# Long-range rows with one maximum, a score bank lent to the projections, and keys in 1024-column tiles

## Chip, cores and metric

The kernel runs on one core of a Trainium2 chip. The metric is device time in microseconds (us) for one execution, lower is better. A time is the median of several runs. A profile is one execution taken by the hardware profiler; its span runs from the first to the last instruction. Engines: PE is TensorE (PEld its weight loads), DVE VectorE, ACT ScalarE, POOL GpSimd, SP SyncE. In this kernel SP issues every DMA.

## What is computed

One layer of a streaming encoder in fp32, for 2048 prompt tokens and 32 sample tokens (with a cache of 128), width 1024. After a norm, one projection gives two groups of attention. Group A ("long-range" here) is differential attention: 4 heads, two query/key maps of 64, values of 128.

```python
s = jnp.einsum('bqhmd,bkhmd->bhmqk', q, k) * (HEAD_DIM ** -0.5) + bias[:, None]
s = jnp.where(mask, s, NEG)
p = jax.nn.softmax(s, axis=-1)
w = p[:, :, 0] - lam * p[:, :, 1]
return jnp.einsum('bhqk,bkhe->bqhe', w, v)
```

The mask is causal by chunks of 64. The bias depends on the distance alone and, once its value for far distances is taken off (softmax does not see it), is zero beyond the last 256 keys of a block of 128 queries. Group B (band) has 8 heads of 64, each chunk attending to itself and 8 chunks before. Then follow an output projection, an MLP of 4096 with a squared ReLU, a gate from a per-layer embedding, and a last norm. New keys and values are outputs too.

## The kernel before

Every fp32 operand of a matmul is split into a high and a low part (`split`, L176 to L187: ACT writes the high part at L181, POOL, L166 and L176, or DVE the low part), and a product takes three matmuls (`mm3`, L216 to L218). Weights come by DMA as `wr`, their parts are `wh` and `wl`.

The code lists work stage by stage. A scheduler with a timeline model puts each engine's instructions into one fixed order, so work of neighbouring stages is interleaved where data and buffers allow; on the chip each engine then runs its list in order. Tiles come from pools with a fixed number of buffers, and a write to a reused buffer waits for its last reader.

PSUM has eight banks of 128 x 512 fp32. Before the change: `mm`, 2 banks, for projections and MLP (`vps`, `qps`, `ups`, `dps`); `pss`, 3 banks (tag `s`), for scores of both groups (`s` at L638, `sb` at L835); `pst`, 2 banks, for transposes (`tpp`, L713); `pso`, 1 bank, for attention outputs (`o`, L727 to L729).

The order of `run`: token preparation with the first value tiles; query and key projections of group A for tokens 0 to 1023; the first long-range part `JA0` (pairs of query tiles 0 to 3, `self.small` true); projections and band rows for all tokens, and group A's second half; the second long-range part `JA1` (pairs 4 and 5, then 6 and 7 with the samples); output projection, MLP, gate and final norm. In the trace the first long-range part runs between 187 and about 480 us beside projections of group B, the second between 1215 and about 1990 beside output projection and MLP of tokens 0 to 1023.

`attn_a` loops over the 4 heads. For each it loads the bias block `ba` (`bias_a`), and the keys of the head, high and low part on 64 partitions each, into one tile `ka` of 1024 columns (first part) or 2048 (second part) with two buffers; then it calls `attn_a_pair` for each pair of 128-query tiles.

`attn_a_pair` handles the two query tiles, for each of the two maps m:

- The keys are cut into blocks: the last 256 columns are the near block, what lies before it is cut evenly into far blocks of up to 512. For each block two matmuls (high and low part) make the scores.
- A far block: DVE takes the negated maximum out of PSUM (L644), and ACT computes exp out of PSUM into SBUF with the block's own maximum and sum (L652). A near block: DVE adds the bias, writes to SBUF and takes the maximum (L647), flips the sign (L650), and ACT takes the exp from SBUF.
- After all blocks: the least of the negated maxima (L657), a correction factor for each block by an exp on ACT (L659), and five small DVE operations (L662 to L666) that give each block its factor.
- For each block ACT scales map 1's weights (L674) and DVE combines the maps (L675). PE transposes the row, ACT (L720) and DVE (L721) take it out as high and low part, and three matmuls per 128 keys make the output. `e0` has two buffers, `e1` two in the first part and one in the second.

The band rows use three `s` banks, an addition with maximum on DVE (L838) and one exp per row.

Of the kernel before, what the change touches and what calls it, by code (L numbers as in the profile page):

```python
# [13 lines left out]
F32 = mybir.dt.float32  # L14
# [6 lines left out]
P = 128  # L21
D = 1024
SP = 2048
# [120 lines left out]
class Kern:  # L144
# [75 lines left out]
    def rsqrt(self, pool, src, n, scale, eps, eng, tag="rs", np_=P, bufs=None, out=None):  # L220
        nc = self.nc
        v = pool.tile([P, n], F32, tag=tag + "v", bufs=bufs, name="rsv")[:np_]
# [102 lines left out]
    def bias_a(self, pool, h):  # L325
        nc = self.nc
        t = pool.tile([P, 256], F32, tag="ba", bufs=1, name="ba")
        src = self.dba[h, 127 : 127 + P * 383].rearrange("(p c) -> p c", c=383)[:, :256]
        self.dma(t, src)
        nc.gpsimd.memset(t[0:64, 192:256], NEG)  # L330
        return t
# [240 lines left out]
    def attn_a(self, js, pool, ps_s, ps_t, ps_o):  # L572
# [4 lines left out]
        for g in range(4):  # L577
            ba = self.bias_a(pool, g)
            kt = pool.tile([P, 2, 1024 if self.small else SP], F32R, tag="ka", bufs=2, name="ka")
            if last:  # L580
                ks = pool.tile([P, 2, PAST + SS], F32R, tag="ks", bufs=1, name="ks")
            for hl in range(2):
                src = self.kS[g, hl].rearrange("(m r) c -> r m c", m=2)
                for c0 in range(0, nk, 1024):
                    c1 = min(c0 + 1024, nk)
                    self.dma(kt[64 * hl : 64 * hl + 64, :, c0:c1], src[:, :, c0:c1])
                if last:
                    self.dma(ks[64 * hl : 64 * hl + 64], src[:, :, SP:KC])
            for j in js:
                self.attn_a_pair(g, j if j < 8 else None, kt if j < 8 else ks, ba, pool, ps_s, ps_t, ps_o, late)  # L590
                if self.small:
                    late.pop(0)()
# [3 lines left out]
    def attn_a_pair(self, g, j, kt, ba, pool, ps_s, ps_t, ps_o, late):  # L596
# [11 lines left out]
        for qi, t in enumerate(tiles):  # L608
            if samp:
                nr = SS  # L610
                blocks = [(SP, PAST + SS, 0)]
                kb = SP
                nkeys = PAST + SS
            else:
                nr = P
                kb = 0
                nkeys = P * (t + 1)
                nfar = max(nkeys - 256, 0)
                nb = (nfar + 511) // 512
# [8 lines left out]
            e = [  # L628
                pool.tile([P, 2048 if not self.small else 1024], F32, tag=f"e{m}", bufs=2 if m == 0 or self.small else 1, name="e")
                for m in range(2)  # L630
            ]
            nm = pool.tile([P, 2, 8], F32, tag="nm", bufs=2, name="nm")
            z = pool.tile([P, 2, 8], F32, tag="z", bufs=2, name="z")
            for bi, (k0, n, near) in enumerate(blocks):
                for m in range(2):
                    s = ps_s.tile([P, 512], F32, tag="s", name="s")[:nr, :n]
                    for hl in range(2):
                        nc.tensor.matmul(  # L638
                            s, q[:, m, hl, P * qi : P * qi + nr], kt[:, m, k0 - kb : k0 - kb + n], start=hl == 0, stop=hl == 1
                        )  # L640
                    dst = e[m][:nr, k0 - kb : k0 - kb + n]
                    nmx = nm[:nr, m, bi : bi + 1]
                    if near is None:
                        nc.vector.tensor_reduce(nmx, s, axis=AX.X, op=ALU.max, negate=True)  # L644
                        src = s
                    else:
                        nc.vector.tensor_tensor_reduce(  # L647
                            dst, s, ba[:nr, near : near + n], 1.0, -3e38, ALU.add, ALU.max, nmx
                        )
                        nc.vector.tensor_scalar(nmx, nmx, -1.0, None, op0=ALU.mult)  # L650
                        src = dst
                    nc.scalar.activation(dst, src, AF.Exp, bias=nmx, accum_out=z[:nr, m, bi : bi + 1])  # L652
            c = pool.tile([P, 2, 8], F32, tag="c", bufs=2, name="c")
# [1059 lines left out]
```

## Time and profile before

| | |
|---|---|
| median of 3 runs | 3140.01 us (3138.12 to 3142.35) |
| the profiled execution's own time | 3143.18 us |
| its span | 3141.4 us |
| mean granted TensorE clock | 0.984 |
| DMA | 539.27 MB, mean 172 GB/s |

A stage is a window of time; a row of the stage view gives the window, its length, then the busy time of each engine in it with the count of instructions, the granted TensorE clock, the DMA share and the rate. A row of a group view gives line, engine, operation, output and input tiles and count, then busy time and mean ns of one, then how long the engine was idle just before them and what ended that. A row of the wait view reads "waiter <- releaser: us in total, times, longest". Busy matmuls overlap in the pipeline, so a PE at 100% is not PE at its peak rate.

### The profile page before, as it was taken

How to read it: one execution, taken by the hardware profiler on the slowest of the kernel's cores; microseconds unless marked ns; L12 is line 12 of the kernel's file. 1: busy time of each engine (PE TensorE's matmuls, PEld its weight loads, DVE VectorE, ACT ScalarE, POOL GpSimd, SP SyncE). 2: the span in 40 equal slices, each digit the busy share in tenths (PEclk: the TensorE clock that was granted, in tenths of full speed). 3: DMA queues.
4: the chain of work that ended last, by engine and by line, in shares of the span. 5: the costliest groups of instructions: out<-in, count | busy, mean ns of one | idle time of the engine just before them, and what ended most of it. 6: DMA issues, size and time to landing. Idle time of an engine off the chain costs nothing. (4 is left out here: it accounts for less than half of the span.)

```text
span 3141.4 us, 52810 instructions
## 1 busy us (share of the span) xinstructions
PE 3009.3 (96%) x17913; PEld 2651.0 (84%) x17913; DVE 1897.7 (60%) x4596; ACT 1876.7 (60%) x4166; POOL 1841.0 (59%) x2496
## 2 busy tenths in 40 slices
PE   8999898999999999999999999999899999999998
PEld 7787787999977887878788888878788888999998
DVE  5147774645465654676756656435667885576653
ACT  5257775766676764776666657454555455554545
POOL 2357455332345644665655545667877888767674
PEclk9999899999999999999999999999999999999999
DMA  8788757986788746555563543537533446333231
GB/s 275 244 239 249 207 185 231 266 230 202 205 251 231 221 126 155 156 152 151 164 191 116 145 123 109 157 98 247 174 128 115 144 153 227 124 107 107 88 116 56
DMA packets 523286, 539.27 MB, mean 172 GB/s; under 512 B 38748, under 2 KB 401568, under 8 KB 523016
## 3 DMA queue, kind: packets, MB, share of 16 engines
q1 hardware_dynamic: 523016, 535.89, 56.6%
q8 instruction: 142, 2.33, 0.3%
q14 instruction: 128, 1.05, 0.1%
HBM read 421.97 MB, written 117.75 MB: 172 GB/s over the span
## 5 line engine op out<-in xcount | busy, mean ns | idle before, releaser
L176 POOL TENSOR_TENSOR wl<-wr,wh 128x256 fp32r<-128x256 f32 x648 | 474.4, 764 | 360.3 <-ACT wh L181 326.7
L181 ACT ACTIVATE piece<-wr 128x512 fp32r<-128x512 f32 x406 | 245.6, 625 | 270.3 <-PE ups L217 107.1
L176 POOL TENSOR_TENSOR piece<-wr,piece 128x256 fp32r<-128x256 f32 x404 | 327.5, 836 | 101.8 <-ACT piece L181 79.8
L181 ACT ACTIVATE wh<-wr 128x1024 fp32r<-128x1024 f32 x228 | 241.0, 1057 | 175.5 <-PE qps L217 41.3
L166 POOL TENSOR_TENSOR wl<-wr,wh 128x256 fp32r<-128x256 f32 x264 | 198.0, 781 | 196.4 <-ACT wh L181 186.3
L216 PE MATMUL dps<-uh,piece 128*128 128x272 f32 (+1 forms) x768 | 246.4, 324 | 6.7 <-DVE h L1221 2.5
L166 POOL TENSOR_TENSOR piece<-wr,piece 128x256 fp32r<-128x256 f32 x280 | 236.1, 874 | 26.6 <-ACT piece L181 25.5
L218 PE MATMUL dps<-uh,piece 128*128 128x272 f32 (+1 forms) x768 | 247.1, 324 | 1.6 <-POOL piece L166 1.5
L216 PE MATMUL ups<-cs,piece 128*128 128x256 f32 (+1 forms) x864 | 245.7, 285 | 1.6 <-DVE r L1232 1.6
L217 PE MATMUL dps<-ul,piece 128*128 128x272 f32 (+1 forms) x768 | 247.2, 323 | 0.0
L217 PE MATMUL ups<-cs,piece 128*128 128x256 f32 (+1 forms) x864 | 245.7, 285 | 0.0
L218 PE MATMUL ups<-cs,piece 128*128 128x256 f32 (+1 forms) x864 | 245.5, 284 | 0.0
L216 PE MATMUL qps<-aH,wh 128*128 128x512 f32 (+1 forms) x640 | 231.7, 362 | 7.7 <-DVE ql L476 3.8
L218 PE MATMUL qps<-aH,wl 128*128 128x512 f32 (+1 forms) x640 | 229.7, 359 | 0.0
L217 PE MATMUL qps<-aL,wh 128*128 128x512 f32 (+1 forms) x640 | 229.0, 358 | 0.0
L1173 DVE TENSOR_TENSOR h<-h,dps 128x512 f32<-128x512 f32 x256 | 174.2, 682 | 84.9 <-PE dps L218 79.2
L1221 DVE TENSOR_TENSOR h<-h,dps 128x272 f32<-128x272 f32 (+1 forms) x384 | 189.0, 513 | 51.6 <-PE dps L218 50.8
L216 PE MATMUL dps<-uh,wh 128*128 128x512 f32 x512 | 208.7, 408 | 9.6 <-DVE h L1173 5.3
L216 PE MATMUL ups<-cH,wh 128*128 128x512 f32 x512 | 202.8, 396 | 1.8 <-DVE h L1173 1.7
L218 PE MATMUL dps<-uh,wl 128*128 128x512 f32 x512 | 202.3, 395 | 0.0
L217 PE MATMUL dps<-ul,wh 128*128 128x512 f32 x512 | 201.8, 394 | 0.0
L638 PE MATMUL s<-ka,q 128*128 128x512 f32 (+3 forms) x768 | 187.1, 346 | 15.0 <-ACT e L652 7.1
(317 smaller groups left out, 9619.0 us busy)
## 6 DMA issues: line engine op xcount, KB each, us to landing
wr<-w_up SPq DMA_DIRECT2D x128, 512.0 KB, 3.9
wr<-w_down SPq DMA_DIRECT2D x128, 512.0 KB, 3.8
wr<-w_in SPq DMA_DIRECT2D x74, 512.0 KB, 5.5
q<-qS SPq DMA_DIRECT2D x128, 256.0 KB, 5.2
v<-vSa SPq DMA_DIRECT2D x64, 512.0 KB, 4.0
ka<-kS SPq DMA_DIRECT2D x32, 512.0 KB, 8.4
wr<-w_out SPq DMA_DIRECT2D x32, 512.0 KB, 4.5
wr<-w_ple_gate SPq DMA_DIRECT2D x32, 512.0 KB, 4.2
```

What stands on the lines that cost most here:

```text
L166: nc.gpsimd.tensor_tensor(out[:, sl], a[:, sl], b[:, sl], op=op)
L176: nc.gpsimd.tensor_tensor(out[:, sl], a[:, sl], b[:, sl], op=op)
L181: nc.scalar.activation(hi, raw, AF.Copy)
L216: nc.tensor.matmul(ps, lh, rh, start=start and i == 0, stop=False)
L217: nc.tensor.matmul(ps, lh, rl, start=False, stop=False)
L218: nc.tensor.matmul(ps, ll, rh, start=False, stop=stop and i == n - 1)
L638: nc.tensor.matmul(s, q[:, m, hl, P * qi : P * qi + nr], kt[:, m, k0 - kb : k0 - kb + n], start=hl == 0, stop=hl == 1)
L1173: nc.vector.tensor_tensor(hv, hv, ps, op=ALU.add)
L1221: nc.vector.tensor_tensor(hv, hv, ps, op=ALU.add)
```

## The change

1. **One maximum for a long-range row.** Blocks are now cut at multiples of 512. A far block is copied from PSUM to SBUF by one DVE `tensor_scalar` that also takes the maximum; the last block adds the bias as before, over its whole width, so the bias tile `ba` grows to 512 columns, the first 256 zero (one more memset on POOL). A last block of 128 columns is joined with the one before and the two are cut 384 and 256. A small reduction gives the row's maximum, and one exp on ACT per map runs over the whole row in SBUF with one sum. The per-block factors go; the scaling and combining of the maps run over up to 1024 columns at once. The loop now takes all blocks of one map before the next map.
2. **A bank moves.** `pss` gets 2 banks instead of 3; the eighth bank is a third one for the projections (`mmx`) until the second long-range part, where it becomes a third score bank (`psy`). The band rows and the ring of the token preparation use two score banks throughout.
3. **Keys in tiles of 1024 columns.** In the second part a head's keys lie in two tiles of 1024 columns, from three buffers, in place of one tile of 2048 from two. A score block that crosses a tile's edge is made by two pairs of matmuls.
4. `e1` has two buffers in the second part too; the variance tile of a norm shares a buffer with `sq`.

```diff
     def bias_a(self, pool, h):
-        t = pool.tile([P, 256], F32, tag="ba", bufs=1, name="ba")
+        t = pool.tile([P, 512], F32, tag="ba", bufs=1, name="ba")
...
+        self.dma(t[:, 256:512], src)
+        nc.gpsimd.memset(t[:, 0:256], 0.0)
+        nc.gpsimd.memset(t[0:64, 448:512], NEG)
...
-            kt = pool.tile([P, 2, 1024 if self.small else SP], F32R, tag="ka", bufs=2, name="ka")
+            kts = [pool.tile([P, 2, 1024], F32R, tag="ka", bufs=2 if self.small else 3, name="ka") for _ in range(0, nk, 1024)]
...
+                nb = -(-nkeys // 512)
                 blocks = []
-                pos = 0
                 for i in range(nb):
-                    n = P * ((nfar // P - pos // P + nb - i - 1) // (nb - i))
-                    blocks.append((pos, n, None))
-                    pos += n
-                blocks.append((nfar, nkeys - nfar, 256 - (nkeys - nfar)))
+                    n = min(512, nkeys - 512 * i)
+                    blocks.append((512 * i, n, None if i < nb - 1 else 512 - n))
+                if nb > 1 and n == P:
+                    blocks[-2:] = [(512 * nb - 1024, 384, None), (512 * nb - 640, 256, 256)]
...
-            for bi, (k0, n, near) in enumerate(blocks):
-                for m in range(2):
+            for m in range(2):
+                for bi, (k0, n, near) in enumerate(blocks):
...
                     if near is None:
-                        nc.vector.tensor_reduce(nmx, s, axis=AX.X, op=ALU.max, negate=True)
-                        src = s
+                        nc.vector.tensor_scalar(dst, s, 0.0, -3e38, op0=ALU.add, op1=ALU.max, accum_out=top)
                     else:
...
-                        nc.vector.tensor_scalar(nmx, nmx, -1.0, None, op0=ALU.mult)
-                        src = dst
-                    nc.scalar.activation(dst, src, AF.Exp, bias=nmx, accum_out=z[:nr, m, bi : bi + 1])
...
+                nmx = nm[:nr, m : m + 1]
+                nc.vector.tensor_reduce(nmx, mx[:nr, m, :nb], axis=AX.X, op=ALU.max, negate=True)
+                row = e[m][:nr, :nkeys]
+                nc.scalar.activation(row, row, AF.Exp, bias=nmx, accum_out=z[:nr, m : m + 1])
+            nc.vector.reciprocal(c[:nr], z[:nr])
+            nc.vector.tensor_scalar(c[:nr, 1:2], c[:nr, 1:2], self.nlam[:nr], None, op0=ALU.mult)
+            for k0 in range(0, nkeys, 1024):
+                sl = slice(k0, min(k0 + 1024, nkeys))
+                nc.scalar.activation(e[1][:nr, sl], e[1][:nr, sl], AF.Copy, scale=c[:nr, 1:2])
                 nc.vector.scalar_tensor_tensor(
...
+            mmx = ExitStack()
+            mz = mm
+            mm = Rings((mz, "mm"), (mz, "mm"), (opened(mmx, "mmx", 1, PSUM), "mm"))
...
-            ps_s = opened(psx, "pss", 5 - MM, PSUM, "right")
+            ps_s = opened(psx, "pss", 4 - MM, PSUM, "right")
...
+            mmx.close()
+            mm = mz
+            ps_y = opened(psx, "psy", 1, PSUM, "right")
+            sy = Rings((ps_s, "s"), (ps_s, "s"), (ps_y, "s"))
...
-                    self.attn_a(js, pool, ps_s, ps_t, ps_o)
+                    self.attn_a(js, pool, sy, ps_t, ps_o)
```

The built kernel after the change has 17,796 matmuls, the one before 17,908.

More of the change, by code (lines that the diff above doesn't have):

```diff
@@ L583, in attn_a @@
                 src = self.kS[g, hl].rearrange("(m r) c -> r m c", m=2)
[L584 to L586 removed]
+                for i, kt in enumerate(kts):
+                    c0, n = 1024 * i, min(1024, nk - 1024 * i)
+                    self.dma(kt[64 * hl : 64 * hl + 64, :, :n], src[:, :, c0 : c0 + n])
                 if last:
@@ L627, in attn_a_pair @@
             nb = len(blocks)
             e = [
[L629 removed]
+                pool.tile([P, 2048 if not self.small else 1024], F32, tag=f"e{m}", bufs=2, name="e")
                 for m in range(2)
             ]
[L632 to L640 removed]
+            mx = pool.tile([P, 2, 4], F32, tag="mx", bufs=2, name="mx")
```

64 lines of the change are left out of this document (23 added, 41 removed).

## The prediction

> **What bounds the kernel now.** I read the page's first part, then busy time by stage, then the waits of TensorE stage by stage.
>
> ```profile
> span 3141.4 us, 52810 instructions
> PE 3009.3 (96%) x17913; PEld 2651.0 (84%) x17913; DVE 1897.7 (60%) x4596; ACT 1876.7 (60%) x4166; POOL 1841.0 (59%) x2496
> ```
>
> TensorE (PE) is busy 96% of the span, so an edit gains only where it closes PE's gaps: 3141.4 - 3009.3 = 132 us in all, and time run at a lowered clock. Next, busy time by stage (columns: window, length, then busy us of PE, PEld, DVE, ACT, POOL with counts, granted clock, DMA share, GB/s).
>
> ```profile
> 0.00:185.00 185.00, 166.87 (x942) 140.83 (x943) 65.08 (x185) 73.15 (x184) 64.99 (x99) 0.97 0.79 254
> 185.00:560.00 375.00, 340.74 (x2018) 296.29 (x2017) 258.20 (x857) 264.70 (x763) 211.70 (x313) 0.94 0.77 224
> 560.00:1200.00 640.00, 622.66 (x3820) 551.58 (x3819) 362.69 (x1224) 430.85 (x892) 274.06 (x413) 0.99 0.73 211
> 1200.00:2000.00 800.00, 778.90 (x3988) 655.62 (x3987) 501.97 (x1123) 515.06 (x1192) 446.23 (x631) 0.99 0.51 146
> 2000.00:3141.40 1141.40, 1100.14 (x7153) 1006.67 (x7151) 709.73 (x1208) 592.96 (x1138) 844.00 (x1043) 0.99 0.42 137
> ```
>
> The long-range rows lie in 185 to 560 (first part, query pairs 0 to 3, with band projections between them) and in 1200 to 2000 (second part, with the MLP between them). The band rows and projections lie in 560 to 1200. The first part is the worst stage: PE is idle 375 - 340.7 = 34.3 us, and a clock of 0.94 costs up to 0.06 x 375 = 22.5 us, 57 us together at most, since idle time at a low clock counts in both. The second part is idle 21.1 us in 800, the band stage 17.3 in 640. Inside the first part:
>
> ```profile
> 185.00:280.00 95.00, 91.08 (x580) 81.27 (x579) 64.85 (x242) 64.10 (x195) 64.87 (x94) 1.00 0.92 256
> 280.00:400.00 120.00, 104.79 (x611) 91.31 (x610) 93.72 (x293) 91.34 (x278) 60.59 (x88) 0.89 0.74 213
> 400.00:560.00 160.00, 144.87 (x831) 123.71 (x830) 99.62 (x323) 109.26 (x294) 86.25 (x133) 0.95 0.70 213
> ```
>
> From 280 to 400 VectorE (DVE) is busy 93.7 of 120 us and ScalarE (ACT) 91.3: both queues are near full, and PE falls behind them. Its waits from 185 to 560 (columns: us in total, times, longest) say whom it waits for:
>
> ```profile
> PE s L638 <- ACT e L652: 7.1, 9, 3.0
> PE rp L392 <- DVE xt L387: 4.5, 3, 2.5
> PE s L638 <- DVE nm L647: 2.5, 3, 1.1
> PE tpp L713 <- DVE e L675: 2.3, 5, 1.1
> ```
>
> The largest is a score matmul waiting until an exp has read the bank (L652). The others are small drains of PSUM late behind DVE's queue. No wait is long; there are many.
>
> **The change part by part.** *One maximum per row.* Before, every block of up to 512 keys had its own maximum and its own exp out of PSUM; afterwards DVE copies the block to SBUF with its maximum, and one exp runs over the whole row.
>
> ```profile
> L652 ACT ACTIVATE e<-s,nm 128x512 f32<-128x512 f32 (+3 forms) x256 | 155.2, 611 | 66.2 <-DVE nm L644 55.4 <-DVE e L675 10.4
> L652 ACT ACTIVATE e<-e,nm 128x256 f32<-128x256 f32 (+2 forms) x136 | 67.3, 496 | 43.2 <-DVE nm L650 42.9
> L652 ACT ACTIVATION_READ_ACCUMULATOR e<-s,nm 128x1 f32 x256 | 52.2, 204 | 0.0
> L652 ACT ACTIVATION_READ_ACCUMULATOR e<-e,nm 128x1 f32 (+1 forms) x136 | 26.3, 193 | 0.0
> L659 ACT ACTIVATE c<-nm,gm 128x2 f32<-128x2 f32 (+3 forms) x112 | 26.7, 290 | 3.3 <-DVE gm L657 3.2
> L674 ACT ACTIVATE e<-e,c 128x384 f32<-128x384 f32 (+4 forms) x196 | 102.8, 586 | 51.7 <-DVE c L666 44.4 <-DVE c L671 6.8 <-DVE nm L650 0.3
> L181 ACT ACTIVATE wh<-wr 128x1024 fp32r<-128x1024 f32 x228 | 241.0, 1057 | 175.5 <-PE qps L217 41.3 <-DMA wr<-w_down 24.5 <-issue 24.4
> L181 ACT ACTIVATE piece<-wr 128x512 fp32r<-128x512 f32 x406 | 245.6, 625 | 270.3 <-PE ups L217 107.1
> ```
>
> ACT before: 155.2 + 67.3 + 52.2 + 26.3 + 26.7 + 102.8 = 430.5 us. The two L181 rows give (1057 - 625) / 512 = 0.84 ns per element; 496 ns at 256 columns leaves a base of 0.28 us. Afterwards there are 136 exps over 140,500 columns in all (8 times 128, 256 ... 2048, and the samples): 136 x 0.28 + 118 = 156 us, 136 reads x 0.2 = 27, and 100 copies over half those columns: 28 + 59 = 87. That is 270, so ACT loses 160 us, by columns about 50 of them in the first part.
>
> DVE, rows by shape over the whole run:
>
> ```profile
> L644 DVE TENSOR_REDUCE nm<-s 128x1 f32<-128x512 f32 x104 | 69.8, 683 | 25.6 <-PE s L638 25.0
> L647 DVE CUSTOM_DVE_ANT_0 e<-s,ba 128x256 f32<-128x256 f32 x120 | 49.2, 417 | 46.3 <-PE s L638 44.9 <-POOL ba L330 0.8 <-PE tpp L713 0.2
> L675 DVE SCALAR_TENSOR_TENSOR e<-e,c 128x512 f32<-128x512 f32 x52 | 44.5, 868 | 12.5 <-ACT e L674 12.4
> L650 DVE TENSOR_SCALAR nm<-nm 128x1 f32<-128x1 f32 x128 | 18.2, 147 | 1.1
> ```
>
> The new far operation (add, maximum, copy out of PSUM) is not in the trace. It lies between the reduction of the same size, 0.68, and L675, which also writes 512, 0.87; I take 0.75, nearer the reduction, since it reads the same bank with one source. 192 of them replace 256 reductions, 128 row maxima replace 128 sign flips (L650), and most of the small coefficient operations go. I put DVE at -40 us in the first part and -40 in the second (-20 to -60 each).
>
> What this is worth where PE waits: in the first part a bank is now freed by DVE alone, the L652 wait goes, and both queues get shorter by some 40 to 50 us in 375. In the built kernel's instruction order 1207 projection matmuls stand between the first and the last matmul of the first part, 989 before. Those 218 are worth, by the rate of a dense window,
>
> ```profile
> 2060.00:2080.00 20.00, 20.00 (x89) 16.46 (x88) 4.45 (x7) 9.50 (x14) 14.09 (x20) 1.00 0.34 105
> ```
>
> 20 / 89 = 0.225 us each, up to 49 us of work that can fill what are gaps today. Bounds: 0 (the first part merely stretches by the added filler) to -57 (all of its loss). Gaps that come from the token preparation (L392) and from DMA stay, so I take half: **-28**. Of the 57, the 22.5 are read off the granted clock, though no wait of PE above is longer than 3.0 us. The Trainium skill ("TensorE: Matmul & The Clock Gate", Part 1) says that the clock halves only after an idle window of about 3.4 us; the trace's 0.94 beside a longest wait of 3.0 does not agree. By that rule the clock's part would not be there to win and the same half would give -17.
>
> *TensorE.* The built kernel has 17,796 matmuls against 17,908, over the same number of columns. If the time goes by columns, nothing is saved; if each instruction counts in full, 112 x 0.225 = 25 us. I take it near 0, since what is streamed stays. **-1**.
>
> *A score bank goes to the projections until the second part.* Three projection banks stand against two, two score banks against three, for band rows too. From 560 to 1200:
>
> ```profile
> PE sb L835 <- DVE stb L838: 4.2, 5, 3.0
> PE qps L216 <- ACT kn L506: 3.5, 1, 3.5
> PE ops L216 <- ACT oact L181: 2.3, 1, 2.3
> ```
>
> A third bank can take the projections' 3.5 + 2.3 and some of the shorter clock dips; a lost score bank can double or triple the 4.2. Bounds -15 to +15; I take **0**. The order of the token preparation's ring hardly matters: it alternates two rings of two, where the score ring had three.
>
> *Keys in 1024-column tiles, three buffers.* Before, a head's keys lay whole in one of two buffers. Now the second tile of a head needs the buffer of the previous head's first tile, which is read to the end of that head. SP, which issues every DMA, waits for that last reader with the next queries and weights queued behind it.
>
> ```profile
> ka<-kS SPq DMA_DIRECT2D x24, 512.0 KB, 8.6
> q<-qS SPq DMA_DIRECT2D x32, 256.0 KB, 4.3
> DMA to landing us min/median/max: 5.6/8.9/13.7
> PE s L638 <- DMA q<-qS: 3.5, 4, 1.8
> ```
>
> In the built order six of the seven reloads have 32 to 60 matmuls between the old tile's last reader and the new tile's first: 7 to 13 us at 0.225. The landing of 8.6 was measured with four such DMAs at once; now two go together, nearer the minimum of 5.6. So a reload costs between 0 and about 4 us: 0 to +24. I take +1 each, **+5** net of the query waits they overlap.
>
> *Longer instructions in the second part.* There PE waits for the queues, not for their sum:
>
> ```profile
> PE dps L216 <- DVE h L1173: 5.3, 7, 1.3
> PE o L727 <- ACT pH L720: 5.8, 3, 2.7
> L1173 DVE TENSOR_TENSOR h<-h,dps 128x512 f32<-128x512 f32 x200 | 135.9, 682 | 55.5 <-PE dps L218 54.0
> ```
>
> An MLP down accumulator takes 6 matmuls, 1.35 us, and two banks alternate. L675 at 1024 columns is 0.87 + 512 x 1.04 ns = 1.4 us by DVE's slope between 256 and 512 in the L647 and L644 rows ((683 - 417) / 256 = 1.04); with L1173's 0.68 behind it, 2.1 us, up to 0.75 over 1.35. 36 of these: 0 to +27. An exp of 2048 takes 0.28 + 1.73 = 2.0 us against a mean of 0.61 today and can hold up a transposed block's evacuation (L720). ACT and DVE together do less work, so gaps may also shrink: -10 at the other end. I take **+3**.
>
> The second bias half costs one memset of 256 columns per head on POOL, 59% busy; the second `e1` buffer removes a wait of ACT for L675 (10.4 in the L652 row). 0 for both; nothing on PE waits for them first.
>
> Sum: -28 - 1 + 0 + 5 + 3 = -21. The profiled execution took 3143.18 us around its span of 3141.4, so 3122; the median of the three runs is 3140.01, 3.2 less, so **3119** for a median.
>
> **The rivals.**
> *All of the first part's loss goes*: DVE and ACT are what holds it. -57 and the filler's 49 bound it; with +8 elsewhere, 3140 - 45 = 3095. For it: the two queues' 78% and 76% from 280 to 400. Against: L392 and DMA shares of 0.92 from 185.
> *Nothing moves* (the change does not do what it says for PE): 96% busy stays, the first part stretches by its filler and the gaps turn up in the band stage, short of filler. 3134 to 3146.
> *Slower: long instructions in the second part.* DVE's and ACT's queues run in order, so every MLP drain behind a 1024-column L675 or a 2048-column exp is late: 36 x 0.75 = 27, plus 64 exps (32 rows, two maps) of a mean 1.6 us (0.28 + 1600 x 0.84 ns) against 0.61: if one in two holds up a transposed block, 64 x 0.5 x 1.0 = 32. With the key reloads at 2 us each, +12, and the first part at -28: +42, 3182; at half these rates +6, 3146. It decides from about 30 us of new gaps in 1200 to 2000. For it: the L1173 and L720 waits lead this stage. Against: the stage's DVE is busy 63% and ACT 64%, and more filler stands between a row's last score and its first transpose. The Trainium skill ("Perfetto Trace Analysis", Optimizing Scalar/DVE Operations) sides with it: where those engines are not saturated but cause bubbles on others, breaking instructions up may let work complete sooner. By that rule the second part should lose; the trace agrees as far as ACT's 64% and PE's waits go.
>
> **How the numbers follow.** A measurement of this kernel tells about 0.2% (6.3 us) from no change: below 3133.7 is faster, above 3146.3 slower. Forecast, 3105 to 3134: 0.52. All the loss goes, 3080 to 3105: 0.16. Nothing moves: 0.15. Slower, to 3180: 0.17. Faster 0.52 + 0.16 = 0.68, same 0.15, slower 0.17. The range 3090 to 3150 leaves out about 0.05 below and 0.14 above.
>
> **What would show it.** Right: from 185 to 560 PE's idle time near 17 us or less and a clock of 0.97; ACT's total near 1720 us; no score wait on an exp there; in the second part waits of score matmuls for key DMAs of 1 us a head. Wrong: the first part ends later by as much filler as it took; `dps` waits for DVE well over 5.3 us, or `o` and score waits of tens of us from 1200 to 2000; PE waits on `sb` growing from 4.2 to over 15.

## The result, and the profile after

The changed kernel takes 3119.46 us, a median of 4 runs (3116.1 to 3121.14), beside 3141.18 us for four runs of the kernel before (3138.12 to 3147.81): the ratio is 0.9923, with a 95% interval of 0.9907 to 0.994. The forecast was 3119, so the sum was right. Its terms were not, as the runs below show: the closing of gaps was put too high, the bank, put at nothing, brought the largest share, and the key tiles cost more than was taken. That these errors cancel is luck.

The profiled execution after took 3116.1 us around a span of 3114.0, at a mean granted clock of 0.986 (0.984 before). First the page's first part:

```profile
span 3114.0 us, 51781 instructions
PE 2992.9 (96%) x17801; PEld 2639.7 (85%) x17801; DVE 1815.1 (58%) x4404; ACT 1779.4 (57%) x3446; POOL 1859.1 (60%) x2512
```

Span and PE's busy time fell by 27.4 and 16.4 us, so PE's gaps closed by only 11. By stage, columns as in the prediction:

```profile
0.00:185.00 185.00, 172.97 (x1023) 148.75 (x1024) 71.83 (x214) 79.58 (x199) 66.23 (x101) 1.00 0.85 270
185.00:560.00 375.00, 344.14 (x2086) 302.30 (x2085) 230.44 (x715) 234.02 (x546) 224.88 (x328) 0.96 0.78 228
560.00:1200.00 640.00, 619.76 (x3707) 546.61 (x3707) 356.84 (x1208) 433.63 (x892) 283.56 (x431) 0.99 0.71 208
1200.00:2000.00 800.00, 778.66 (x3943) 653.25 (x3943) 467.04 (x1084) 453.33 (x699) 466.99 (x647) 0.99 0.54 152
```

PE's idle time changed most in the first stage: 12.0 us instead of 18.1, with 1023 matmuls instead of 942 and a clock of 1.00 instead of 0.97. The first score comes at 176.2 instead of 186.5. The first long-range part, on which the prediction rested, is idle 30.9 us instead of 34.3, at 0.96 instead of 0.94. The band stage, 560 to 1200, is idle 20.2 us instead of 17.3. The inner windows of the first part:

```profile
280.00:400.00 120.00, 108.96 (x656) 95.73 (x656) 76.81 (x217) 76.67 (x170) 73.53 (x104) 0.97 0.76 225
400.00:560.00 160.00, 143.89 (x880) 126.14 (x879) 92.83 (x295) 96.65 (x227) 80.11 (x120) 0.93 0.68 206
```

From 280 to 400 DVE went from 93.7 to 76.8 us, ACT from 91.3 to 76.7, and the clock from 0.89 to 0.97, as expected. From 400 to 560 PE has 16.1 us of gaps (15.1 before) and a lower clock than before. PE's waits from 185 to 560, then from 1200 to 2000:

```profile
PE sb L820 <- DMA q<-qS: 6.2, 2, 4.7
PE o L712 <- ACT pH L705: 4.7, 2, 4.3
PE rp L393 <- DVE rcol L231: 4.4, 1, 4.4
PE s L639 <- DVE e L646: 3.2, 3, 1.4
```

```profile
PE s L639 <- DMA q<-qS: 9.7, 4, 3.8
PE dps L216 <- ACT relu L1123: 4.4, 2, 4.0
PE dps L216 <- DVE h L1158: 2.1, 4, 0.8
```

No score waits for an exp in the first part any more. In its place stand fewer and longer waits. In the second part the queries' DMA comes late, 9.7 us against 3.5. The band scores of 560 to 1200 wait 7.7 us for DVE (`sb`, 4.2 before), short of the 15 that the prediction named as a sign of being wrong.

The changed operations, by shape and then by line:

```profile
L646 DVE TENSOR_SCALAR_CACHE_REDUCE e<-s 128x512 f32<-128x512 f32 x168 | 112.2, 685 | 45.9 <-PE s L639 29.0 <-PE tpp L698 16.6
L646 DVE DVE_READ_ACCUMULATOR e<-s 128x1 f32 x192 | 15.6, 81 | 0.0
L660 DVE SCALAR_TENSOR_TENSOR e<-e,c 128x1024 f32<-128x1024 f32 x40 | 56.5, 1415 | 27.5 <-ACT e L659 27.5
L654 ACT ACTIVATE e<-e,nm 128x2048 f32<-128x2048 f32 x8 | 16.1, 2008 | 2.7 <-DVE nm L652 2.7
```

```profile
L654 ACT ACTIVATE e<-e,nm 128x128 f32<-128x128 f32 (+16 forms) x136 | 157.1, 1156 | 97.4 <-DVE nm L652 96.9
L654 ACT ACTIVATION_READ_ACCUMULATOR e<-e,nm 128x1 f32 (+1 forms) x136 | 25.4, 187 | 0.0
L659 ACT ACTIVATE e<-e,c 128x1024 f32<-128x1024 f32 (+6 forms) x100 | 84.3, 874 | 15.6 <-DVE c L656 13.4 <-DVE nm L652 1.8
```

Each duration is near its estimate: the far copy with maximum 0.685 us (0.75 assumed) with 0.081 for its result, the 1024-column combination 1.415 (1.4), the 2048-column exp 2.008 (2.0).

### The profile page after: what moved, and what is told of

Read it like the earlier page. It is cut to its first block, busy times and chain, and to the rows that moved or that the text cites. A ratio compares the mean times of both kernels' runs of the same rounds, so it can differ in the third digit from the quotient of the medians.

```text
span 3114.0 us, 51781 instructions
## 1 busy us (share of the span) xinstructions
PE 2992.9 (96%) x17801; PEld 2639.7 (85%) x17801; DVE 1815.1 (58%) x4404; ACT 1779.4 (57%) x3446; POOL 1859.1 (60%) x2512
## 5 line engine op out<-in xcount | busy, mean ns | idle before, releaser
L176 POOL TENSOR_TENSOR wl<-wr,wh 128x256 fp32r<-128x256 f32 x648 | 482.3, 776 | 322.6 <-ACT wh L181 271.2
L166 POOL TENSOR_TENSOR wl<-wr,wh 128x256 fp32r<-128x256 f32 x264 | 197.2, 777 | 166.9 <-ACT wh L181 162.0
L654 ACT ACTIVATE e<-e,nm 128x128 f32<-128x128 f32 (+16 forms) x136 | 157.1, 1156 | 97.4 <-DVE nm L652 96.9
```

What stands on the lines that cost most here:

```text
L166: nc.gpsimd.tensor_tensor(out[:, sl], a[:, sl], b[:, sl], op=op)
L176: nc.gpsimd.tensor_tensor(out[:, sl], a[:, sl], b[:, sl], op=op)
L654: nc.scalar.activation(row, row, AF.Exp, bias=nmx, accum_out=z[:nr, m : m + 1])
```

## The experiments

All were timed in several rounds against the kernel before, whose median on those chips was 3148 to 3149 us; so ratios are compared, and a step between two ratios is turned into us by 3141. One ratio is known to about 0.0013, so a step between two of them to about 5 or 6 us. Every variant is laid out anew by the scheduler, whose order is part of what is measured, and no run changed the order alone.

One profiled execution can stand several us from its median: that of the kernel before took 3143.2 us, 5 to 6 less than its median beside the variants. So what is gained is read from the ratios; the profiles only show where.

The clearest reading is one window for each kernel, from 0 to the first `yp` matmul, the start of the final norm of tokens 0 to 1023. All long-range and band rows lie before it, and what follows took 1052 to 1061 us in every kernel here (1055.2 before, 1054.6 after). This spread of 9 us lies in work that no variant is about, so steps of 8 to 10 us below stand on weaker ground than their intervals say. The columns are those of the stage view. Before, and after:

```profile
0.00:2086.20 2086.20, 1993.20 (x11124) 1712.91 (x11125) 1224.58 (x3437) 1324.54 (x3091) 1064.09 (x1547) 0.98 0.65 190
```

```profile
0.00:2059.40 2059.40, 1974.85 (x11012) 1699.32 (x11013) 1144.76 (x3245) 1226.64 (x2371) 1084.13 (x1563) 0.99 0.66 193
```

PE's idle time is the length less its busy time: 93.0 before, 84.6 after. So of the 26.8 us, 8.4 are idle time and 18.4 are less time in matmuls: 112 fewer of them, and a clock of 0.99 instead of 0.98.

### The bank alone

The kernel before with the third projection bank, two score banks until the second part, and nothing else.

```diff
+            mmx = ExitStack()
+            mz = mm
+            mm = Rings((mz, "mm"), (mz, "mm"), (opened(mmx, "mmx", 1, PSUM), "mm"))
-            ps_s = opened(psx, "pss", 5 - MM, PSUM, "right")
+            ps_s = opened(psx, "pss", 4 - MM, PSUM, "right")
...
+            mmx.close()
+            mm = mz
+            ps_y = opened(psx, "psy", 1, PSUM, "right")
+            sy = Rings((ps_s, "s"), (ps_s, "s"), (ps_y, "s"))
-                    self.attn_a(js, pool, ps_s, ps_t, ps_o)
+                    self.attn_a(js, pool, sy, ps_t, ps_o)
```

> The kernel before with the bank alone moved: three projection banks and two score banks up to the second long-range part, score blocks, per-block maxima and keys as before. Theory of the prediction (the shorter ACT and DVE queues of the one maximum close the first part's gaps): the bank is worth nothing, 3134 to 3147 us, and the first score starts near 186 us as before. Rival A (the third projection bank closes gaps of the projections, from the start of the kernel): 3115 to 3128 us, the first score near 176 us as in the changed kernel. Rival B (the order of the scheduler shifts by some 10 us with any edit): a change of either sign of up to 10 us, not in the places where the changed kernel gains.

Measured: 3184.53 us, ratio 1.0123 (1.0106 to 1.014). Slower by 38.6 us, which none of the three sides had. Three windows of it, the start, the band stage and the end of the second part; then the start in the kernel before:

```profile
0.00:175.00 175.00, 165.27 (x950) 140.15 (x950) 65.57 (x186) 74.12 (x185) 66.08 (x100) 1.00 0.85 270
560.00:1200.00 640.00, 604.02 (x3482) 520.24 (x3481) 354.21 (x1207) 427.96 (x886) 262.10 (x413) 0.99 0.74 209
2050.00:2100.00 50.00, 35.67 (x158) 28.45 (x159) 22.25 (x54) 24.62 (x60) 11.28 (x21) 0.73 0.25 83
```

```profile
0.00:175.00 175.00, 156.87 (x883) 132.09 (x883) 63.05 (x182) 69.62 (x177) 60.54 (x91) 0.97 0.77 251
```

The start is faster: 67 more matmuls by 175 us, and the first score at 175.2 instead of 186.5. All of that is given back later. From 560 to 1200 PE is idle 36.0 us against 17.3, and its wait of band scores is

```profile
PE sb L835 <- DVE stb L838: 18.5, 18, 3.4
```

18.5 us against 4.2. At the end the second part outlasts the MLP beside it. Tile views of this kernel (after the count: shortest, median and longest duration in ns, then first and last start in us):

```profile
L638 PE MATMUL s<-ka,q x768: 220/338/792, 175.2 to 2059.4; 128*128 128x256 f32 x70, 128*128 128x384 f32 x65, 128*128 128x512 f32 x49, 128*128 128x128 f32 x8
L216 PE MATMUL ups<-cH,wh x512: 387/389/504, 1005.5 to 1991.0; 128*128 128x512 f32 x171
```

The last score comes 68 us after the last up-projection. In the kernel before it comes 71 us ahead of it (1961.2 and 2032.1). From 2050 to 2100 PE is busy 35.7 of 50 us at a clock of 0.73.

### A score bank less, and nothing for it

The same with the freed bank idle until the second part: the price of the score bank alone.

```diff
-            ps_s = opened(psx, "pss", 5 - MM, PSUM, "right")
+            ps_s = opened(psx, "pss", 4 - MM, PSUM, "right")
...
+            ps_y = opened(psx, "psy", 1, PSUM, "right")
+            sy = Rings((ps_s, "s"), (ps_s, "s"), (ps_y, "s"))
-                    self.attn_a(js, pool, ps_s, ps_t, ps_o)
+                    self.attn_a(js, pool, sy, ps_t, ps_o)
```

> The kernel before with two score banks instead of three up to the second part and no third projection bank: one bank lies idle till then. The bank alone lost 1.2%. Theory (the projections, with a third bank, are used up early, and the rows that come late run without filler): this does not happen here; within 0.5% of before, first score near 186 us. Rival (two score banks starve rows whose banks are held by exps): 0.8 to 1.5% slower.

Measured: 3182.16 us, ratio 1.0113 (1.0098 to 1.0127), the rival's side. The loss of a score bank costs 35.5 us with the old rows, and in the row up to `yp` 17.7 of it are idle time (110.7 against 93.0):

```profile
0.00:2122.10 2122.10, 2011.45 (x11124) 1723.82 (x11125) 1234.91 (x3437) 1330.64 (x3088) 1064.41 (x1542) 0.97 0.64 187
```

With the old rows the third projection bank then gives nothing (1.0113 to 1.0123). Here too the last score comes late, at 2059.8, after the last up-projection at 2035.1; so that comes already with the lost score bank.

### One maximum alone

Keys whole, one `e1` in the second part, the banks as before.

```diff
-            kts = [pool.tile([P, 2, 1024], F32R, tag="ka", bufs=2 if self.small else 3, name="ka") for _ in range(0, nk, 1024)]
+            kt = pool.tile([P, 2, 1024 if self.small else SP], F32R, tag="ka", bufs=2, name="ka")
...
-                pool.tile([P, 2048 if not self.small else 1024], F32, tag=f"e{m}", bufs=2, name="e")
+                pool.tile([P, 2048 if not self.small else 1024], F32, tag=f"e{m}", bufs=2 if m == 0 or self.small else 1, name="e")
...
-            ps_s = opened(psx, "pss", 4 - MM, PSUM, "right")
+            ps_s = opened(psx, "pss", 5 - MM, PSUM, "right")
```

(against the changed kernel; the projections' third bank and `psy` go as well)

> The changed kernel with the banks and the key tiles of before: one maximum per row alone (with one e1 buffer in the second part). Theory of the prediction: it brings most of the gain, 3112 to 3124 us, by the end of the first part. Rival A (the bank brings it): 3132 to 3146 us. By the profile's landmark of 10 us gained before the first score, which no score instruction can explain, a split is expected: about 3125 with the first score at 186 us.

Measured: 3133.01 us, ratio 0.9947 (0.9935 to 0.996): 16.6 us faster. The first score is at 185.3, so the early start of the changed kernel (176.2) is the bank's. Up to `yp`:

```profile
0.00:2081.40 2081.40, 1984.78 (x10995) 1704.39 (x10996) 1141.48 (x3245) 1228.74 (x2371) 1080.68 (x1563) 0.98 0.65 191
```

PE idles 96.6 us, no less than before (93.0); its matmuls, 129 fewer at the same clock of 0.98, take 8.4 us less. These two profiles differ by 7.9 us in their spans (3141.4 and 3133.5), half of the 16.6 by ratio, so where the other half lies is not shown. From 175 to 560 the gaps did shrink, from 34.3 to 30.8 us, but in the band stage they grew, as the rival "nothing moves" had it for the whole change:

```profile
560.00:1200.00 640.00, 616.02 (x3740) 546.22 (x3741) 345.84 (x1164) 412.52 (x838) 265.83 (x404) 0.98 0.72 207
```

24.0 us idle there against 17.3. The first part also ends earlier: the first band score, which follows it, is at 472.1 instead of 512.4. In this profile the rows run faster, and the time is partly lost in the next stage.

### One maximum and the bank, keys whole

```diff
+            mmx = ExitStack()
+            mz = mm
+            mm = Rings((mz, "mm"), (mz, "mm"), (opened(mmx, "mmx", 1, PSUM), "mm"))
-            ps_s = opened(psx, "pss", 5 - MM, PSUM, "right")
+            ps_s = opened(psx, "pss", 4 - MM, PSUM, "right")
```

(against the kernel of the last run, with the lines at the second part as in "the bank alone")

> The changed kernel with whole-head key tiles in two buffers and one e1 buffer in the second part, as before: one maximum and the bank without the key tiles. Theory: the key tiles cost some 5 us of waits in the second part, so this is 3112 to 3118 us. Rival (reloads land in time, and smaller bursts of key DMAs help the weights): 3119 to 3126 us, with more idle time of PE from 1200 to 2000 us than the 21 us of the changed kernel.

Measured: 3113.51 us, ratio 0.9885 (0.9872 to 0.9899), the fastest of all; faster than the changed kernel, as the theory had it, and by more. Beside one maximum alone the bank is worth 0.62%, 19.5 us. Up to `yp`:

```profile
0.00:2055.30 2055.30, 1975.69 (x10995) 1699.79 (x10996) 1156.34 (x3245) 1228.45 (x2371) 1085.24 (x1563) 0.99 0.66 193
```

79.6 us idle, 17.0 less than with one maximum alone, and 9.1 us less in the same 10,995 matmuls, beside a clock of 0.99 instead of 0.98.

### One maximum, a score bank less, and nothing for it

```diff
-            ps_s = opened(psx, "pss", 5 - MM, PSUM, "right")
+            ps_s = opened(psx, "pss", 4 - MM, PSUM, "right")
...
+            ps_y = opened(psx, "psy", 1, PSUM, "right")
+            sy = Rings((ps_s, "s"), (ps_s, "s"), (ps_y, "s"))
-                    self.attn_a(js, pool, ps_s, ps_t, ps_o)
+                    self.attn_a(js, pool, sy, ps_t, ps_o)
```

> One maximum with whole keys and two score banks up to the second part, the freed bank idle, two projection banks. The kernel before loses 1.1% by the lost score bank. Theory (with one maximum a bank is freed by DVE alone, so a third score bank is hardly missed): within 0.3% of one maximum alone, 0.993 to 0.997. Rival (a score bank is worth as much as before, and only the third projection bank makes up for it): 1.002 to 1.006.

Measured: 3163.53 us, ratio 1.0051 (1.0037 to 1.0065). The score bank is worth 1.04%, 33 us, with one maximum too: the rival's side. So the rows need the third score bank as much as before, and it is the third projection bank that changes its worth: 1.66%, 52 us, with one maximum (1.0051 to 0.9885), nothing with the old rows. First 175 to 560 here, then in the kernel with maximum and bank:

```profile
175.00:560.00 385.00, 345.78 (x1990) 297.36 (x1989) 229.42 (x725) 236.73 (x553) 219.84 (x327) 0.94 0.78 223
```

```profile
175.00:560.00 385.00, 356.82 (x2171) 314.65 (x2170) 236.76 (x742) 240.50 (x561) 226.36 (x331) 0.96 0.79 230
```

181 matmuls more, and 64 more from 0 to 175 (876 and 940). In the band stage 81 of these are given back (3770 and 3689). With the old rows the same step was 75 and 214 more, and 206 given back (3688 and 3482 in the band stage).

### The bank lent only until the first long-range part

One maximum, whole keys; the bank returns to the scores before the first part.

```diff
+            mmx.close()
+            mm = mz
+            tp = mm
+            ps_y = opened(psx, "psy", 1, PSUM, "right")
+            ps_s = Rings((ps_s, "s"), (ps_s, "s"), (ps_y, "s"))
...
-            mmx.close()
-            mm = mz
-            ps_y = opened(psx, "psy", 1, PSUM, "right")
-            sy = Rings((ps_s, "s"), (ps_s, "s"), (ps_y, "s"))
-                    self.attn_a(js, pool, sy, ps_t, ps_o)
+                    self.attn_a(js, pool, ps_s, ps_t, ps_o)
```

> One maximum, whole keys, and the third projection bank only up to the first long-range part; from there two projection banks and three score banks as before. Theory (the bank is worth 10 us before the first score and the rest by letting projections run beside the long-range rows): first score near 176 us, 3.3 us per thousand of the gain lost against the full loan: ratio 0.991 to 0.993. Rival (after the first score a third score bank is worth as much): 0.986 to 0.989.

Measured: 3119.32 us, ratio 0.9915 (0.9901 to 0.9929), in the theory's range. The first score is at 176.0, as with the whole loan. So of the 19.5 us some 10 come from the start (0.9947 to 0.9915), and 9 from the loan during first part and band rows, each known to about 6 us.

### Key tiles alone

```diff
-            kt = pool.tile([P, 2, 1024 if self.small else SP], F32R, tag="ka", bufs=2, name="ka")
+            kts = [pool.tile([P, 2, 1024], F32R, tag="ka", bufs=2 if self.small else 3, name="ka") for _ in range(0, nk, 1024)]
```

(against the kernel before, with the split of a score block at a tile's edge)

> The kernel before with its keys in 1024-column tiles from three buffers in the second part, and nothing else. Theory: +2 to +10 us, waits of score matmuls for key DMAs at the head changes. Rival (nothing is late): within 4 us of before.

Measured: 3151.9 us, ratio 1.001 (1.0001 to 1.0019): +3 us. That lies in the theory's range and in the rival's, so the run does not decide between them; it is near the +5 of the prediction. With the old rows the tiles cost little, and from 1200 to 2060 scores wait 0.9 us for queries, less than before.

### The changed kernel again, and its parts

Beside the runs with a second `e1`, the changed kernel once more:

> The changed kernel itself, beside the variants. Against the kernel with one maximum and the bank but whole key tiles (ratio 0.9885): if the key tiles with their reloads cost what the prediction gave them (+5 us), 0.990; by its first measurement 0.9923.

Measured: 3121.86 us, ratio 0.9918 (0.9905 to 0.993). It lies 0.33% behind maximum and bank with whole keys (0.38% by the first measurement): 10 to 12 us lost through key tiles and `e1` together. One `e1` buffer in the changed kernel:

```diff
-                pool.tile([P, 2048 if not self.small else 1024], F32, tag=f"e{m}", bufs=2, name="e")
+                pool.tile([P, 2048 if not self.small else 1024], F32, tag=f"e{m}", bufs=2 if m == 0 or self.small else 1, name="e")
```

> The changed kernel with one e1 buffer in the second part, as before; three key tiles as changed. Theory (the 10 us that the changed kernel lacks against whole keys and one e1 buffer, 0.9885 to 0.992, are key reloads): as the changed kernel, 0.990 to 0.993. Rival (the second e1 buffer lets long-range rows crowd out the MLP's drains): 0.988 to 0.989, as with whole keys.

Measured: 3129.61 us, ratio 0.9944 (0.993 to 0.9958), slower than both sides had. Against whole keys, with one `e1` in both (0.9885), the three tiles cost 0.59%, 18.5 us. And that kernel with a fourth key tile, so that no reload waits for the previous head's first tile:

```diff
-            kts = [pool.tile([P, 2, 1024], F32R, tag="ka", bufs=2 if self.small else 3, name="ka") for _ in range(0, nk, 1024)]
+            kts = [pool.tile([P, 2, 1024], F32R, tag="ka", bufs=2 if self.small else 4, name="ka") for _ in range(0, nk, 1024)]
```

> The same with a fourth buffer for key tiles, so that no reload waits for the previous head's end; the space equals that of whole keys in two buffers. Theory (reloads cost): 0.987 to 0.9895, some 5 to 10 us below the run with three. Rival (the extra matmuls at tile edges or the split loads cost): no better than three tiles.

Measured: 3119.52 us, ratio 0.9913 (0.9896 to 0.993), between the two. The fourth tile is worth 0.31%, 10 us (intervals that touch). Four tiles are still 0.28%, 9 us, behind whole keys in as many bytes and with 16 matmuls more; how much of it is the scheduler's order was not taken apart. The second `e1` is worth some 8 us (0.9944 to 0.9918, intervals that touch). SP's waits from 1200 to 2060 for a score matmul, the reader that a key or query reload waits for, with three tiles and one `e1`, then with four:

```profile
SPq L157 <- PE s L639: 44.2, 15, 7.9
```

```profile
SPq L157 <- PE s L639: 28.0, 12, 5.8
```

SP stands 16 us less in such waits. But PE does not wait less for what SP brings: scores wait for queries 2.0 us with three tiles and one `e1`, 2.9 with four, 2.6 with whole keys. It is with the second `e1` that they wait 9.7 and 8.9 us (the two profiles of the changed kernel), and that kernel is the faster one. Also, 7.0 of the 13.2 us between the profiles of three and four tiles lie behind the first `yp`, where no key tile is read. So the fourth tile's 10 us are not shown to be reloads that PE waits for.

### A second `e1` with whole keys

What the key tiles pay for: whole keys, maximum, bank, and a second `e1`.

```diff
-                pool.tile([P, 2048 if not self.small else 1024], F32, tag=f"e{m}", bufs=2 if m == 0 or self.small else 1, name="e")
+                pool.tile([P, 2048 if not self.small else 1024], F32, tag=f"e{m}", bufs=2, name="e")
```

> One maximum and the bank, keys whole in two buffers, and the second e1 buffer in the second part as in the changed kernel: the changed kernel without the key tiles alone. Theory (the key tiles' reloads are what the changed kernel lacks against whole tiles): ratio 0.987 to 0.990. Rival (the second e1 buffer lets the rows run ahead and crowds the MLP's drains): 0.991 to 0.993.

Measured: 3458.04 us, ratio 1.0979 (1.0959 to 1.1): 9.8% slower than the kernel before, and 11% slower than the same with one `e1`, which neither side had. The up-projection of the MLP, here and in the kernel with one `e1`:

```profile
L216 PE MATMUL ups<-cH,wh x512: 387/389/793, 1634.1 to 2351.8; 128*128 128x512 f32 x171
```

```profile
L216 PE MATMUL ups<-cH,wh x512: 387/389/506, 995.4 to 2004.9; 128*128 128x512 f32 x171
```

It begins at 1634.1 instead of 995.4: the MLP no longer lies beside the second part, and PE is bare there.

```profile
1400.00:1600.00 200.00, 135.75 (x643) 106.61 (x642) 116.63 (x296) 100.06 (x172) 53.16 (x79) 0.77 0.39 112
```

By the tiles' sizes: two whole key buffers hold 2 x 2 x 2048 x 4 bytes = 32 KB a partition, three tiles of 1024 hold 24 KB, and a second `e1` takes 2048 x 4 = 8 KB. The key tiles pay for `e1` to the byte. That the MLP's buffers found no room is argued from this, not measured by itself.

### Short steps

The changed kernel with exp, scaling and combination in steps of 512 columns and a small sum of the exps' parts.

```diff
+            zp = pool.tile([P, 2, 4], F32, tag="zp", bufs=2, name="zp")
...
-                row = e[m][:nr, :nkeys]
-                nc.scalar.activation(row, row, AF.Exp, bias=nmx, accum_out=z[:nr, m : m + 1])
+                for i, k0 in enumerate(range(0, nkeys, 512)):
+                    row = e[m][:nr, k0 : min(k0 + 512, nkeys)]
+                    nc.scalar.activation(row, row, AF.Exp, bias=nmx, accum_out=zp[:nr, m, i : i + 1])
+                nc.vector.tensor_reduce(z[:nr, m : m + 1], zp[:nr, m, : i + 1], axis=AX.X, op=ALU.add)
...
-            for k0 in range(0, nkeys, 1024):
-                sl = slice(k0, min(k0 + 1024, nkeys))
+            for k0 in range(0, nkeys, 512):
+                sl = slice(k0, min(k0 + 512, nkeys))
```

> The changed kernel with the row's exp, and the scaling and combining of the maps, in steps of 512 columns instead of the whole row and 1024; one maximum per row stays, the partial sums are added by one small reduction. Rival of the prediction (long instructions block the queues of ACT and DVE): faster than the changed kernel by 5 to 20 us, 0.985 to 0.990. Theory (queue work matters, and 512 more columns' bases of 0.28 us each on ACT cost): 0.993 to 0.998.

Measured: 3136.64 us, ratio 0.9961 (0.9948 to 0.9975): slower than the changed kernel by 0.43%, 13 us. The time is in the theory's range, and the rival falls. From 1200 to 2060 the waits of `dps` for DVE are

```profile
PE dps L216 <- DVE h L1161: 5.0, 6, 2.5
```

5.0 us, against 2.1 with long steps: short steps do not bring the drains forward.

## Why the prediction was right, and where its steps were not

| step | predicted | measured | from |
|---|---|---|---|
| one maximum, with fewer matmuls and longer instructions | -28 - 1 + 3 = -26 | -17 | one maximum alone |
| the bank | 0 (-15 to +15) | -19.5 | with it less without it, one maximum in both |
| key tiles, second `e1` | +5 (0 to +24) | +10 to +12 | changed kernel less maximum and bank |
| sum | -21 | -24 to -26 | (0.9923 and 0.9918) |

The steps are taken in this order, each kernel less the one ahead of it. With the bank first they would be +38.6 for the bank and -75 for one maximum (1.0123 to 0.9885): the two are worth what they are only together.

- **"I take half: -28" was too much.** The first steps came: no score waits for an exp, DVE and ACT have gaps again from 280 to 400, the clock there is up, and the first part of one maximum alone lasts 287 us from first score to first band score instead of 326. But the test that was set for it fails: idle time of 17 us and a clock of 0.97 from 185 to 560 were asked for, 30.9 and 0.96 were found. In the profile of one maximum alone PE idles as long up to `yp` as before. The gaps moved: the band stage lost what the first part gained, and in the changed kernel waits for queries, for the transposed block's evacuation (L705) and for the token preparation, of 4.3 to 4.7 us each, took the place of many short ones. So the rival "nothing moves" was half right about idle time. What remained in this profile is PE's own time, 8.4 us up to `yp` with 129 fewer matmuls. The term for TensorE, -1, was then probably too small, but no run changed the count of matmuls alone.

- **The bank at 0 failed in kind, not in size.** The prediction priced the third projection bank by waits in the band stage, 560 to 1200, and looked at no wait ahead of 185, where the projections have nothing else beside them. There the bank gives 52 to 75 matmuls more by 175 us, whichever two kernels with and without it are compared. It also took a gain and a loss of at most 15 us each. With one maximum they are about 33 lost and 52 gained, far larger than any wait that the profile names (4.2, 3.5, 2.3): a bank's worth was not to be read off the waits that are there while one has it.

- **Gain and loss depend on the rows.** With the old rows the same edit costs 38.6 us. The table has PE's idle time by stage in us (length less busy time in each profile), for the banks of scores and projections until the second part:

  | rows | score, projection banks | 0 to 175 | 175 to 560 | 560 to 1200 | 1200 to `yp` | ratio |
  |---|---|---|---|---|---|---|
  | old | 3, 2 | 18.1 | 34.3 | 17.3 | 23.3 | 1 |
  | old | 2, 2 | 18.4 | 33.8 | 25.4 | 33.0 | 1.0113 |
  | old | 2, 3 | 9.7 | 23.5 | 36.0 | 43.5 | 1.0123 |
  | one maximum | 3, 2 | 17.6 | 30.8 | 24.0 | 24.2 | 0.9947 |
  | one maximum | 2, 2 | 18.9 | 39.2 | 24.1 | 28.5 | 1.0051 |
  | one maximum | 2, 3 | 10.3 | 28.2 | 22.6 | 18.5 | 0.9885 |

  Up to 560 the third projection bank closes the same gaps with both kinds of rows, some 9 us before 175 and 10 to 11 us after. What differs comes behind: with the old rows about 21 us of new gaps, with one maximum 11 us fewer. The counts of matmuls above go the same way: with the old rows 206 of the 289 that were done early are missing in the band stage, with one maximum 81 of 245. So it fits that projections done early are filler that later stages lack. That this decides it is argued. The length of the first part, from first score to first band score, does not decide it alone: with one maximum and two score banks it lasts 329 us without the third projection bank and 346 with it, and the longer one is faster by 52 us. That a far block now holds its bank only through one DVE copy, and no longer through DVE's reduction and ACT's exp, does not explain it by itself either: a score bank should then have become cheaper, and it costs 33 us as it did 35.5. Each variant has another order on every engine, and no run kept the order and changed the bank alone.

- **Key tiles and `e1`.** The sum of +10 to +12 hides two errors: with one `e1` the tiles cost 18.5 us, where +5 was taken (0 to +24), and the second `e1`, taken at 0, gives back some 8. The mechanism that was named (reloads behind the last reader on SP, queries queued behind them) is not shown. A fourth tile takes 16 us off SP's waits and gives 10 us back, but PE's waits for queries do not follow: 2.0 us where the tiles cost 18.5, and 9.7 in the changed kernel, which is faster. No waits of scores for key DMAs of "1 us a head" came either. Up to `yp` the kernel with three tiles and one `e1` has 8.1 us more idle time and 6.9 us more time in matmuls than the one with whole keys (2070.2 us with 1982.5 busy, against 2055.3 with 1975.7); what makes them stays open.

- **Long instructions: wrong sign.** They were taken as a small loss (+3), and as the rival on the slower side. Short steps are 13 us slower. The Trainium skill ("Perfetto Trace Analysis", Optimizing Scalar/DVE Operations) says that breaking instructions up may help where those engines cause bubbles without being saturated; ACT and DVE stood at 57 and 58%, and here it did not help. Short steps also cost ACT and DVE more time, 1838.4 and 1853.7 us against 1779.4 and 1815.1; that this is the cause was not tested by itself.

- **ACT's total** was to be near 1720 and is 1779. The price by rows was right: 266.8 us (157.1 + 25.4 + 84.3) where 270 was worked out, 430.5 before. But the page's total fell by 97 only, not by 164. Rows count each instruction's whole time, and the total counts overlapping ones once; the 256 short reads of accumulators that went had lain partly beside their neighbours. DVE, with -80 predicted, fell by 82.6.

- **The clock.** In the changed kernel the two deepest dips after 400 lie where PE waits longest: clock 0.83 from 420 to 440 (the wait of 4.3 for L705 lies between 400 and 440) and 0.66 from 520 to 540 (the 4.7 for queries, between 500 and 560).

```profile
420.00:440.00 20.00, 15.57 (x96) 14.12 (x95) 13.55 (x46) 11.78 (x31) 3.47 (x6) 0.83 0.53 159
520.00:540.00 20.00, 14.18 (x64) 11.89 (x65) 9.88 (x47) 12.91 (x36) 3.56 (x9) 0.66 1.01 274
```

  The Trainium skill's rule ("TensorE: Matmul & The Clock Gate", Part 1: the clock halves after an idle window of about 3.4 us) fits the length of these two waits, though in the first the clock fell 2.0 us after the wait began (426.4 to 428.4). It does not fit the kernel before, which had 0.89 from 280 to 400 beside waits of at most 3.0. A finer view of the kernel before shows what happens there:

```profile
307.10:310.50 3.40, 1.97 (x9) 1.16 (x9) 3.40 (x9) 3.40 (x11) 3.40 (x6) 1.00 0.38 112
310.50:317.30 6.80, 5.33 (x20) 4.66 (x20) 6.77 (x28) 5.54 (x20) 3.35 (x6) 0.50 1.00 299
```

  PE was busy 1.97 of 3.4 us, with waits of 1.1, 0.4 and 0.3 us, and then the clock stood at half for 6.8 us. The changed kernel has such a case too: busy 1.37 of 3.4 us from 404.5 to 407.9, with waits of 1.4 and 0.7, and a clock of 0.51 in the next 3.4 us. So several short waits close together can cost clock as one long wait does, and the prediction had reason to count the 22.5 us as something to be won.

The best version found is one maximum with the lent bank, whole keys and one `e1` in the second part: 0.9885 (0.9872 to 0.9899), ahead of both kernels.

## What to carry to other kernels

Price a PSUM bank by the stage that would get it and by the stage that would lose it, each with and without, and not by the waits that are seen while all have theirs: here a bank was worth 33 and 52 us beside waits of 2 to 4, and the same loan lost 39 us with the rows of before. When PE is 96% busy, a faster stage may only hand its gaps to the next one, so measure up to a landmark behind both, with idle time and matmul time apart. A smaller tile that pays for another buffer should be measured apart from that buffer: here the tiles cost 18.5 us and the buffer gave back some 8.

## What the runs showed of the hardware

- Copying 512 columns from PSUM to SBUF with a running maximum (685 ns) takes DVE no longer than the reduction alone did (683 ns); the maximum's read adds 81 ns.
- ACT's base and slope held far beyond the shapes they were taken from: 0.28 + 2048 x 0.84 ns gives 2.0 us, and 2.008 was measured.
- One more buffer of 8 KB a partition (a second `e1` with whole keys) moved the MLP's start by 639 us and made the kernel 11% slower (0.9885 to 1.0979).
- The granted clock fell to half for 6.8 us after a stretch of 3.4 us in which PE was busy 1.97 us and no wait was longer than 1.1 us (kernel before, 307.1 to 317.3).
- The 392 reads of ACT's accumulator in the kernel before take 78.5 us as rows (52.2 + 26.3); in its trace all but 9.1 us of that lies beside other instructions of ACT.
